# First FFN groups of both layers: un-normalized input, block products instead of direct ones

## The chip, the cores and the metric

The kernel runs on one core of a Trainium2 chip. The metric is the device time of one launch in microseconds (us); the time of a kernel is the median of its runs.

## The reference

One sequence of 512 tokens with 1024 channels passes two layers, all in float32. A layer is a mixer and a gated ConvFFN, each behind an RMS norm and each added to the residual `h`. The change touches the FFN and the way into it:

```python
def rms_norm(x, g):
    y = x * rsqrt(mean(x * x, axis=-1) + EPS)
    return y * g

def gated_conv_ffn(x, w_gate, w_up, conv_w, conv_b, w_down):   # D_FF = 2816
    g = einsum('bsd,df->bsf', x, w_gate)
    g = causal_dwconv3(g, conv_w) + conv_b        # 3 taps along the tokens, per channel
    up = einsum('bsd,df->bsf', x, w_up)
    return einsum('bsf,fd->bsd', silu(g) * up, w_down)

for layer in range(2):
    h = h + mixer(rms_norm(h, norm_mix[layer]))
    hn = rms_norm(h, norm_ffn[layer])
    h = h + gated_conv_ffn(hn, ...)
```

The factor of the norm is one number per token (`rstd`) and one per channel (`norm_ffn`). It commutes with a product over the channels as far as the token's number goes, so it can be applied to the outputs of `w_gate` and `w_up` instead of to their input.

## The kernel before

**Layout.** Channels lie on the 128 partitions and tokens along the free axis: `h[k]`, k = 0..7, is 128 channels by 512 tokens. For a float32-like result every operand is split into a high and a low half of type fp32r, and each product is three matmuls, high by high, high by low, low by high (`mm3`). The halves of the FFN's input are `hg[k]`, those of weights come from the pools `whi` and `wlo` (6 slots each) and are made from `raw` tiles (4 slots) that the SP queue fetches, 512 KB each. A high half is a rounding copy on ACT. A low half is a subtraction on DVE (`parts`, `halves`), or a negated copy on ACT and an accumulating DMA that POOL issues (`summed`, and kp = 2, 3 in `normalize`).

**Order of work.** The program is written in a tile framework: a planner with its own costs takes each engine's instructions in order of priority (the order of the program text) as their operands and slots become free, and writes one fixed order per engine. `behind` and `inorder` pin some of it. So PE's order also is not that of the text: of two groups of matmuls, the one that the planner sees ready goes first.

**Stages.** mixer 0, its output projection `oe` (two column groups `gi` of 96 matmuls), FFN 0, mixer 1, its output projection `oo`, FFN 1, final norm. `project` takes its residual output block by block: `done` adds a block to `h[k]`, and `Norm.add` makes `hg[k]` as the halves of `h[k]` times the norm weight, and adds the squares up on POOL (`ssq`). The FFN has 22 blocks of 128 hidden channels, taken in groups `f` of two blocks (gate and up, two blocks each). Groups run in parts, and after each part comes the down projection `d` (layer 1: `dn`) over its blocks:

```python
PARTS = (((0, 2), 0, 2), ((4,), 2, 6), ((6, 8), 6, 10), ((10, 12), 10, 14), ...)
```

**A direct group** (`direct`, f = 0 and 2): 4 outputs by 8 k by 3 = 96 matmuls of 512 columns. Group 0 works on `hg` not yet normalized: in its middle `rstd_cols` and `rstd_spread` make `r`, the tokens' `rstd` on all partitions, and its outputs are multiplied by `r` in `evacuate`. While it runs, `normalize(kp)` for the four pairs kp makes the normalized `hg` anew and, from it, the sums and differences of its four blocks (two channel halves by two token halves of 256), with their halves `t23` and `t41`.

**A group in block products** (`both`, all other f): gate and up, each as 7 products of 4 kp by 3 = 12 matmuls of 256 columns (a Strassen form; a plain product in blocks would take 8). Each of the 14 products needs its own stationary halves: `a11`, `s12`, `s34` and the two plain blocks through `summed`, seven slots a group. Results are put together out of PSUM banks a, e, b by copies on ACT and additions on DVE. Then come the convolution (one ACT and two DVE instructions a block), SiLU (ACT), the product with up (DVE) and the halves of the result, `a_hi` (ACT) and `a_lo` (DVE), which are the operands of `d`.

In layer 1 the residual is turned by PE at the start of the FFN (`turn_residual`, tiles `hT`, copied by ACT into `y`), and `t23` lies in the memory of `h`.

## Time and profile before

| what | value |
|---|---|
| median of 3 runs | 994.64 us (994.16 to 994.67) |
| the profiled execution's own time | 994.15 us |
| its span in the profile | 992.4 us |
| PE busy | 982.9 us (99%), 5905 matmuls |
| weight loads (PEld) busy | 875.6 us (88%) |
| DVE busy | 728.5 us (73%) |
| ACT busy | 536.3 us (54%) |
| POOL busy | 105.3 us (11%) |
| FFN 0 begins, first `gu` matmul | 146.13 us |
| FFN 1 begins, first `hT` transpose | 633.84 us |

A line of the profile's timeline has the start, the duration, the engine, the line of the code, the operation, the tiles out<-in, the shapes and a count. In square brackets is how long the engine was idle before, and what released it. A PE duration includes the pipeline, so the pace of matmuls is read from their starts.

### The profile page before, as it was taken

How to read it: one execution, taken by the hardware profiler on the slowest of the kernel's cores; microseconds unless marked ns; L12 is line 12 of the kernel's file. 1: busy time of each engine (PE TensorE's matmuls, PEld its weight loads, DVE VectorE, ACT ScalarE, POOL GpSimd, SP SyncE). 2: the span in 40 equal slices, each digit the busy share in tenths (PEclk: the TensorE clock that was granted, in tenths of full speed). 3: DMA queues.
4: the chain of work that ended last, by engine and by line, in shares of the span. 5: the costliest groups of instructions: out<-in, count | busy, mean ns of one | idle time of the engine just before them, and what ended most of it. 6: DMA issues, size and time to landing. Idle time of an engine off the chain costs nothing.

```text
span 992.4 us, 14934 instructions
## 1 busy us (share of the span) xinstructions
PE 982.9 (99%) x5905; PEld 875.6 (88%) x5905; DVE 728.5 (73%) x1104; ACT 536.3 (54%) x806; POOL 105.3 (11%) x121
## 2 busy tenths in 40 slices
PE   9999999999999999999999999999999999999997
PEld 6788888898999989999888988888989899898996
DVE  6897458967785877858988665399668768687676
ACT  5623346744653746537668634675546366363664
POOL 2141031200000000000300001211000010000100
PEclk9999999999999999999999999999999999999999
DMA  7442225544553645536423513435546456464542
GB/s 246 133 146 85 86 88 131 121 148 118 133 147 97 181 121 132 148 98 180 136 87 93 182 54 97 105 91 130 143 101 159 124 125 173 94 163 126 123 112 85
DMA packets 83073, 125.07 MB, mean 126 GB/s; under 512 B 4308, under 2 KB 56252, under 8 KB 83004
## 3 DMA queue, kind: packets, MB, share of 16 engines
q1 hardware_dynamic: 74028, 98.24, 31.4%
q0 software_dynamic: 7056, 23.60, 13.3%
q10 hardware_dynamic: 1920, 2.30, 0.7%
q8 instruction: 46, 0.75, 0.3%
q14 instruction: 23, 0.19, 0.1%
HBM read 98.42 MB, written 2.10 MB: 101 GB/s over the span
## 4 chain that ended last, share of the span: by engine, by line
PE 94%; issue 1%; DVE 1%; DMA 1%; ACT 0%; DVEq 0%; POOLq 0%; ACTq 0%
PE d L154 4%; PE d L153 4%; PE d L155 4%; PE dn L153 4%; PE dn L154 4%; PE dn L155 4%; PE gu L153 3%; PE gu L154 3%; PE gu L155 3%; PE v L153 1%; PE oo L155 1%; PE oo L153 1%; PE v L155 1%; PE oe L155 1%; PE oe L154 1%; PE v L154 1%
## 5 line engine op out<-in xcount | busy, mean ns | idle before, releaser
L153 PE MATMUL dn<-whi_dn,a_hi 128*128 128x512 f32 (+1 forms) x180 | 69.4, 386 | 0.0
L154 PE MATMUL dn<-wlo_dn,a_hi 128*128 128x512 f32 (+1 forms) x180 | 69.3, 385 | 0.0
L154 PE MATMUL d<-a_lo,whi_d 128*128 128x512 f32 x176 | 68.7, 390 | 0.0
L155 PE MATMUL d<-a_hi,wlo_d 128*128 128x512 f32 x176 | 68.5, 389 | 0.0
L155 PE MATMUL dn<-whi_dn,a_lo 128*128 128x512 f32 (+1 forms) x180 | 67.9, 385 | 0.0
L153 PE MATMUL d<-a_hi,whi_d 128*128 128x512 f32 x176 | 66.9, 390 | 0.0
L566 DVE SCALAR_TENSOR_TENSOR c<-rows,prm,c 128x512 f32<-128x512 f32 x88 | 66.4, 766 | 0.0
L141 POOL DMA_DIRECT2D wlo_g<-raw_g x22 | 19.1, 867 | 373.9 <-ACT wlo_g L140 257.9
L1109 DVE TENSOR_TENSOR y<-dn,y 128x512 f32<-128x512 f32 (+1 forms) x49 | 32.5, 674 | 23.3 <-PE dn L155 23.0
L140 ACT ACTIVATE wlo_g<-raw_g 128x1024 fp32r<-128x1024 f32 x22 | 23.2, 1056 | 42.4 <-PE dn L154 42.4
L572 ACT ACTIVATE s<-c,prm 128x512 f32<-128x512 f32 x44 | 31.7, 720 | 20.5 <-DVE c L566 20.4
L679 DVE TENSOR_TENSOR wlo_s34u<-s34u,whi_s34u 128x1024 fp32r<-128x1024 f32 x18 | 22.0, 1225 | 27.9 <-ACT whi_s34u L678 27.9
L155 PEld LDWEIGHTS dn<-whi_dn,a_lo 128*128 128x128 f32 x180 | 33.8, 188 | 7.3 <-DVE a_lo L262 0.2
L678 ACT ACTIVATE whi_s12u<-s12u 128x1024 fp32r<-128x1024 f32 x18 | 18.9, 1051 | 39.3 <-PE d L154 33.7
L153 PEld LDWEIGHTS dn<-whi_dn,a_hi 128*128 128x128 f32 x180 | 33.8, 188 | 7.0 <-ACT a_hi L260 0.2
L154 PEld LDWEIGHTS dn<-wlo_dn,a_hi 128*128 128x128 f32 x180 | 33.8, 188 | 6.4
L154 PEld LDWEIGHTS d<-a_lo,whi_d 128*128 128x128 f32 x176 | 33.1, 188 | 7.3 <-DVE a_lo L262 0.2
L305 DVE TENSOR_TENSOR h<-d,h 128x512 f32<-128x512 f32 x48 | 32.5, 683 | 9.2 <-PE d L155 9.2
L153 PEld LDWEIGHTS d<-a_hi,whi_d 128*128 128x128 f32 x176 | 32.8, 188 | 7.0
L155 PEld LDWEIGHTS d<-a_hi,wlo_d 128*128 128x128 f32 x176 | 33.0, 188 | 6.7
L260 ACT ACTIVATE a_hi<-s 128x512 fp32r<-128x512 f32 x44 | 27.6, 628 | 16.1 <-DVE s L751 7.4
L149 DVE TENSOR_TENSOR wlo_dn<-raw_dn,whi_dn 128x1024 fp32r<-128x1024 f32 x22 | 26.8, 1220 | 11.6 <-ACT whi_dn L148 11.6
(1274 smaller groups left out, 3469.1 us busy)
## 6 DMA issues: line engine op xcount, KB each, us to landing
raw_g<-in_w_ffn_gate_dram SPq DMA_DIRECT2D x36, 512.0 KB, 4.6
raw_u<-in_w_ffn_up_dram SPq DMA_DIRECT2D x36, 512.0 KB, 4.7
wlo_g<-raw_g POOLq DMA_DIRECT2D x22, 512.0 KB, 4.7
raw_d<-in_w_ffn_down_dram SPq DMA_DIRECT2D x22, 512.0 KB, 4.0
raw_dn<-in_w_ffn_down_dram SPq DMA_DIRECT2D x22, 512.0 KB, 4.0
wlo_u<-raw_u POOLq DMA_DIRECT2D x19, 512.0 KB, 4.6
raw_oe<-in_w_out_even_dram SPq DMA_DIRECT2D x8, 512.0 KB, 3.6
raw_g<-in_w_ffn_gate_dram SPq DMA_DIRECT2D x16, 256.0 KB, 2.9
```

The costliest lines, as they stand in the source:

```text
L140: first = nc.scalar.activation(lo, raw, AF.Copy, scale=-1.0)
L141: nc.gpsimd.dma_start(lo, raw, accum_op=ALU.add)
L149: behind(nc.vector.tensor_tensor(lo, raw, hi.bitcast(F32), ALU.subtract), after[0])
L153: nc.tensor.matmul(ps, lhs[0], rhs[0], start=start, stop=False)
L154: nc.tensor.matmul(ps, lhs[0], rhs[1], start=False, stop=False)
L155: nc.tensor.matmul(ps, lhs[1], rhs[0], start=False, stop=stop)
L260: nc.scalar.activation(hi, src, AF.Copy, scale=scale)
L305: nc.vector.tensor_tensor(h[k], ps, h[k], ALU.add)
L566: nc.vector.scalar_tensor_tensor(c, t[:, i : S + i], prm("cf", i * NF + ft), c, op0=ALU.mult, op1=ALU.add)
L572: nc.scalar.activation(s, c, AF.Silu, bias=self.prm("bf", ft))
L679: nc.vector.tensor_tensor(lo, src, hi.bitcast(F32), ALU.subtract)
L1109: nc.vector.tensor_tensor(dst, ps, dst, ALU.add)
```

## The change

`normalize` goes. In both layers the FFN's products take `hg`, residual times norm weight, to the end, and `r` is applied to outputs in every group. Group 0 keeps its gate direct (48 matmuls of 512) and takes up in 7 block products (84 of 256). Group 2 becomes a group in block products. The weights of group 0 are fetched and prepared from within `project`, ahead of the matmuls of its second column group. In the block sums kp = 0 and 3 go by DVE and kp = 1 and 2 by the accumulating DMA.

```diff
-    def project(name, w, acts, ks, norm, before=None):
+    def project(name, w, acts, ks, norm, before=None, between=None):
...
+            if gi == 1 and between is not None:
+                between()
...
+    def first_weights(layer, into):
+        w = w_ffn_gate[layer][:, : 2 * P].rearrange("(h k p) c -> p h k c", h=2, p=P)
...
+        into["g", 0] = parts(*gate[0])
...
+        halves(w[0][:, 0], w[1][:, 0], r0[:, :, :P])
+        put((2, 4), *parts(*raws["u", 1]))
+        nc.vector.tensor_tensor(a22, a21, a22, ALU.add)
+        nc.vector.tensor_tensor(a21, a11, a21, ALU.subtract)
+        nc.vector.tensor_tensor(a11, a22, a11, ALU.subtract)
+        nc.vector.tensor_tensor(a12, a12, a11, ALU.subtract)
+        put((3, 5), *parts(r1, 4, 2 * P, f"u{layer}_0_s41"))
+        into["g", 1] = parts(*gate[1])
+        put((6, 7), *summed(r0, 4, 2 * P, f"u{layer}_0_s23"))
...
-        def normalize(self, kp):
-            for i, k in enumerate((kp, kp + NP)):
-                nc.vector.scalar_tensor_tensor(x[:, i, :], h[k], self.prm("ffn", k), r, ...)
-            halves(hg[kp], x[:, 0, :])
-            halves(hg[kp + NP], x[:, 1, :])
+        def block_sums(self, kp):
+            nc.scalar.activation(t[:, 2:, :], h[kp]..., AF.Copy, scale=self.prm("ffn", kp))
...
+            for (hi, lo), src in ((self.t41[kp], t[:, 2:, :]), (self.t23[kp], t[:, :2, :])):
+                if kp in (0, 3):
+                    self.summed = halves(hi, lo, src)
                     continue
...
+        def first_up(self, s):
+            for product in (1, 2, 3, 5, 6, 7, 4):
+                ps = self.multiply(banks, f"u{n}", product, self.weights["u", product],
+                                   "c" if product == 3 else None)
...
-        def both(self, f):
+        def products(self, f):
...
-                if (key, product) == ("g", 4):
-                    s[1] = self.silu(self.conv(pads[1], f + 1), f + 1)
-                elif (key, product) == ("g", 3):
-                    s[0] = self.silu(self.conv(pads[0], f), f)
+                if (key, product) in (("g", 4), ("g", 3)):
+                    j = product == 4
+                    row = pads[j][:, 2:]
+                    nc.vector.tensor_tensor(row, row, self.r, ALU.mult)
+                    s[j] = self.silu(self.conv(pads[j], f + j), f + j)
+                    if j:
+                        nc.vector.tensor_tensor(s[1], s[1], self.r, ALU.mult)
...
+            nc.vector.tensor_tensor(kept[:, :2, :], kept[:, :2, :], self.r..., ALU.mult)
             nc.vector.tensor_tensor(s0, kept[:, :2, :], s0, ALU.mult)
...
         def hidden(self, f, before=lambda i, j: None):
+            if f > 0:
+                self.products(f)
+                return
...
+            evacuate = self.first_gate(first)
+            for kp in range(NP):
+                self.block_sums(kp)
+            self.first_up(evacuate())
```

`between` is `first_weights`; its up products stand in the order 1 (`a11`), 2 and 4, 3 and 5, 6 and 7, and only the last pair goes through the accumulating DMA. `block_sums` takes one scaled copy on ACT and four DVE instructions of 256 columns a pair kp, two of which multiply `h[kp + NP]` by its norm weight in passing. In `first_up` products 1, 3 and 7 are copied by ACT and 2, 5, 6 and 7 bring an addition on DVE. `rstd_cols` now stands at step (3, 0) of the gate's matmuls and `rstd_spread` at (4, 1).

`first_gate` is `direct` for the two gate outputs alone; its `evacuate` multiplies by `r` on DVE before the convolution and on POOL after the SiLU, as before. In layer 1 the eight turns of the residual, formerly ahead of the first eight of 32 steps, come ahead of the first eight of 16.

## The prediction

> **What bounds the kernel now.** I read the page first, for the engines' shares and the chain.

> ```profile
> span 992.4 us, 14934 instructions
> ...
> PE 982.9 (99%) x5905; PEld 875.6 (88%) x5905; DVE 728.5 (73%) x1104; ACT 536.3 (54%) x806; POOL 105.3 (11%) x121
> ...
> PE 94%; issue 1%; DVE 1%; DMA 1%; ACT 0%; DVEq 0%; POOLq 0%; ACTq 0%
> ```

> PE carries the chain. A busy PE need not be at its pace, so the waits of PE come next:

> ```profile
> PE clock L62 <- DVE idle L57: 1.3, 1, 1.3
> PE u_20b L535 <- DMA wlo_u<-raw_u: 0.8, 1, 0.8
> PE z L415 <- ACT hgh L392: 0.4, 1, 0.4
> ```

> 2.5 us in all. So there are two ways to change the time: fewer or shorter matmuls, or new waits of PE. The pace is in the timeline of PE (a 512-column run) and in the chain (products of 12):

> ```profile
> 157.08 0.39 PE L153 MATMUL gu<-hgh,whi_u 128*128 128x512 f32 x1
> ...
> 170.23 0.39 PE L154 MATMUL gu<-hgl,whi_g 128*128 128x512 f32 x1
> ```

> ```profile
> 264.25 1.44 PE g_8a L535 x12
> 265.69 1.44 PE u_8a L535 x12
> ...
> 270.01 1.44 PE u_8e L535 x12
> ```

> 58 steps from 157.08 to 170.23 are 0.2267 us for a matmul of 512; 1.44 / 12 is 0.1200 us for one of 256, more than half of the other. That eats much of what seven products instead of eight save. Last, the engines that feed PE, by stretches (down projection 222 to 244, group 6, group 8; then all of the two direct groups):

> ```profile
> 222.11:243.90 21.79, 21.79 (x98) 17.92 (x97) 18.01 (x29) 8.01 (x10) 0.86 (x1) 1.00 0.52 141
> 243.95:264.08 20.13, 20.13 (x169) 20.13 (x168) 12.54 (x20) 11.20 (x18) 1.70 (x2) 1.00 0.37 91
> 264.08:284.31 20.23, 20.23 (x170) 20.20 (x169) 15.49 (x24) 14.43 (x24) 0.85 (x1) 1.00 0.64 176
> ```

> ```profile
> 146.00:191.00 45.00, 45.00 (x206) 37.30 (x205) 37.60 (x66) 30.69 (x47) 10.54 (x10) 1.00 0.51 117
> ```

> After length and PE come PEld, DVE, ACT, POOL. DVE has 46.0 of 62.2 us in a whole part and 37.6 of 45 in the direct groups: room, but at single joints little of it. Two joints in DVE's timeline:

> ```profile
> 268.33 1.22 DVE L679 TENSOR_TENSOR wlo_s12u<-s12u,whi_s12u 128x1024 fp32r<-128x1024 f32 x1
> ...
> 289.83 0.68 DVE L262 TENSOR_TENSOR a_lo<-s,a_hi 128x512 fp32r<-128x512 f32 x1
> ```

> The first ends at 269.55; the product that needs it (u_8e) starts at 270.0. The second ends at 290.5, while `d` runs from 284.3: 24 matmuls over blocks 6 and 7 and three over 9 (27 x 0.2267 = 6.1) cover it to 290.4. And where such a joint is missed now, in the last group of layer 1 (chain):

> ```profile
> 942.24 6.62 issue
> ...
> 948.88 5.94 DMA wlo_u<-raw_u
> ...
> 954.86 1.46 PE u_20b L535 x10
> ```

> The accumulating DMA went out 6.85 us after its group began (942.03); in group 8, which has no wait, it is 5.7 us (269.78 after 264.08).

> **PE's work.** Group 2: 96 x 0.2267 = 21.76 becomes 168 x 0.1200 = 20.16, 1.60 less. Up of group 0: 48 x 0.2267 = 10.88 becomes 84 x 0.1200 = 10.08, 0.80 less. 2.40 a layer, 4.80 in all, and 2 x (36 + 72) = 216 matmuls more. The transposes and the small products for `rstd` stay. I take no error on the paces, since thousands of matmuls keep them. [...]

> **The start of the FFN** (layer 0, from T = 146.13). Gate takes 48 x 0.2267 + 1.17 (`ssc` 0.81, `ssr` 0.36) = 12.05; products 1, 2, 3 need only `hg`. So the sums `t41` are due at T + 16.4 (product 5), `t23` at T + 17.8 (6), group 2 starts at T + 22.1. Ready: the last `hgl` ends at T + 2.7 (148.12 + 0.75). The sums no longer wait for `rstd`, for which DVE idled 2.05 us at 154.4. By the distances of starts (256 columns 0.34, 512 0.60, 1024 1.13) DVE needs 16 x 0.34 + 4 x 0.60 + 1.13 for the gate's second low half + about 1 for `rstd` = 10.0, so it ends at T + 12.7. The pairs by DMA: kp 2 summed at about T + 9, copy 0.6, issue 0.9, landing 4.2 (median on the page), T + 14.7, due with its half of product 5 at T + 17.1: 2.4 us of slack. Of the weights, two slots of six are free when `oe`'s second group starts, and one comes free at 129.8, 135.2, 145.4 and 146.1 as before; the gate's second half gets the fifth, ready near T + 3, due at T + 6.3. The moved DMAs keep their place behind `oe`'s on SP. On POOL the accumulate for products 6 and 7 (0.86) stands near the last `ssq` addition (148.77 to 150.06), for which PE's `ssc` waits at 150.21; two such issues stand around it now (146.96, 150.01), so I charge nothing; in the worst order it is 0.9.

> Then DVE has, up to product u5 of group 2 (T + 27.9): gate outputs 2 x (0.60 + 2 x 0.66), additions 4 x 0.34, the end of up 2 x 0.34 + 3 x 0.60, `a11` 1.2, `s12` of both 2 x 2.33: 13.5 us in 15.2. ACT has about 26 us by T + 35. In layer 1 eight copies of `hT` (0.52 each, 4.2) come on top, while PE's turns put the due times off by 3.5. DVE worked as tightly from 181 to 205 us before, and PE waited nowhere. So 0 to 1.9 us a layer: the upper end uses up the slack by the 2.8 us that ACT waited for DVE's sum at 165.45 and a landing of 5.94 instead of 4.2. I take 0.3, 0.6 in all. A gain beyond PE's has no room: PE does not wait here now.

> **The multiplications by rstd.** Four DVE instructions of 512 columns, 2.4 us, in each of ten groups a layer. DVE's total: +54 busy (80 x 0.68), -23 (normalizing, 16 of each kind at 0.74 and 0.68), about +34 for the new sums and halves: near 793. In a part it is 46.0 + 4.8 of 62: not the bound. First groups of a part prepare during `d`, where DVE idles. Second groups (eight) prepare behind the first group's end, with 0.4 us of slack at u5: 2.4 us late, unless g2 and g7, whose weights are ready (DMA issued 261.6; low half done 267.1), go ahead of it; they give 2.88. Bounds 0 and 1.07 (the pause at u_20b, 0.97 + 0.10, where the joint slipped by 1.15): I take 0.15, as seven of eight joints show under 0.1: 1.2 in all.

> The ten joints from products to `d`: the last `a_lo` comes 1.2 to 2.4 us later. Ready besides: block 9 for three more outputs (9 x 0.2267 = 2.0), and three of the seven banks for the next column group (18 x 0.2267 = 4.1). Bounds 0 and 2.3 each; I take 0.

> **Sum.** -4.8 + 0.6 + 1.2 = -3.0. Against the profiled execution's 994.15 (span 992.4, 1.75 around it) that is 991.15; the median of the runs lies 0.49 above it, so 991.6.

> **Rivals.** (a) *The chain to `d` grows and PE's order doesn't make room.* Place: all ten joints. Two of the four multiplications lie in the last block's own chain, 1.2 us; past a slack of about 0.2 that is 1.0 each: -4.8 + 1.8 + 10 = +7.0, 1001.6. It decides from 0.3 us a joint. For it: the slack is nil as ordered. Against: PE already fills 6 us there, with work to spare. 0.18. (b) *Second groups slip as u_20b did*, all eight by 1.07 (one is there already): -4.8 + 0.6 + 7.5 = +3.3, 997.9. For it: that joint, slipped by half of the 2.4. Against: g2 and g7. 0.10. (c) *The start is late* by 1.9 in both layers: -4.8 + 3.8 + 1.2, 994.8. 0.14. (d) *The pace follows the columns*, 113.3 ns: 19.04 a group, 8.2 saved, 988.2 with the same charges. The rows do not bear it out: 0.02. [...]

> **How the numbers follow.** The forecast has 0.56; its own range is 989.8 (no charge) to 992.6. A measurement can tell about 0.2%, 2.0 us: faster is below 992.65, slower above 996.6. Faster: forecast and (d), 0.58. Same: (c), 0.14. Slower: (a) and (b), 0.28. The range runs from 989.3 (no charge, and half of the 1.07 at u_20b gone) to 1000.0, which takes in (c) and (b) and a joint of 0.8 us in (a), and leaves out the rest of (a) and (d), not quite 0.2.

> **What would show it.** 6121 matmuls, PE busy near 979, DVE near 793. Group 2 begins 22 us after FFN 0's first gate matmul and `d` over blocks 0 and 1 is reached 42.3 after it (44.95 before). PE's waits should name at most `t` or `t23` in the start, `wlo_s12u` or `wlo_u` in second groups, `a_lo` at `d`. Waits of 0.3 us and more at each `d` would prove (a); a start of 46 us would prove (c) and worse.

## The result, and the profile after

The changed kernel takes 1021.75 us (median of 6 runs, 1018.81 to 1024.28), the kernel before 994.65 beside it: a ratio of 1.0274 (95% interval 1.0256 to 1.0292). The profiled execution took 1021.34, 27.19 more than that of before (994.15).

The page after, its head and the chain:

```profile
span 1019.6 us, 15474 instructions
...
PE 990.4 (97%) x6121; PEld 886.2 (87%) x6121; DVE 786.2 (77%) x1210; ACT 548.6 (54%) x828; POOL 109.3 (11%) x123
...
PE 21%; issue 5%; DMA 4%; DVE 2%; ACT 1%; POOLq 0%; DVEq 0%; ACTq 0%; SPq 0%
```

The matmuls are the 6121 that were counted, and DVE is 7 us under what was forecast; PE is busy 11 us more than the 979 that were forecast. And the chain, 94% PE before, now breaks up among other engines. PE's waits say where (engine, what waited, for what: us in all, times, longest):

```profile
PE g_4b L539 <- DMA wlo_g<-raw_g: 3.3, 2, 1.9
PE u_2b L539 <- DMA wlo_u<-raw_u: 2.6, 2, 1.6
PE v L153 <- ACT v L987: 2.2, 1, 2.2
PE u_2a L539 <- DVE wlo_a L556: 1.5, 1, 1.5
...
PE g_4e L539 <- DVE wlo_s12g L556: 1.2, 2, 0.7
PE u_2e L539 <- ACT whi_s12u L555: 1.0, 2, 0.8
PE u_20b L539 <- DMA wlo_u<-raw_u: 1.0, 2, 0.6
PE u_16b L539 <- DMA wlo_u<-raw_u: 0.9, 2, 0.4
```

Group 2 and group 4 wait for their weights' halves, every second group for `wlo_u`, and `v` in mixer 1, whose code is the same, for ACT. No wait at `d` or `dn` is longer than 0.51.

One more thing is new. The view by windows gives the granted clock behind the columns of the engines. In the changed kernel it is 0.50 in two stretches of 3.41 us; before it is 1.00 from 5.2 to 985.4, as long as matmuls run:

```profile
216.90:220.30 3.40, 3.40 (x18) 3.40 (x18) 1.23 (x1) 1.42 (x2) 0.00 (x0) 0.50 1.11 205
534.35:537.75 3.40, 3.40 (x10) 2.62 (x9) 3.40 (x6) 3.40 (x8) 0.00 (x0) 0.50 0.00 0
```

In them matmuls of 256 columns start 0.213 us apart instead of 0.120, those of 512 0.427 instead of 0.227, so 1.5 to 1.6 us of each are lost. They begin right behind waits of PE: 0.42 at `u_4e` and 1.32 at `g_4b` in the 3.4 us ahead of the first, 2.21 at `v` ahead of the second.

Where the 27.2 us lie is read from PE's timeline, stage by stage. "Start" runs from group 0's first gate matmul to `d` over blocks 0 and 1, "4" from there to `d` over blocks 2 to 5 (so it holds 10.9 us of `d`, and group 4), "parts" from there to `v` or to the end of the last matmul. All are us of the profiled execution.

| kernel | start 0 | 4 | parts | mixer 1 | start 1 | 4 | parts, end | median of runs |
|---|---|---|---|---|---|---|---|---|
| before | 44.95 | 31.03 | 270.81 | 141.27 | 48.13 | 31.03 | 272.21 | 994.65 |
| after | 49.89 | 35.77 | 274.26 | 145.33 | 51.16 | 34.89 | 275.43 | 1021.75 |
| e1 no multiplications | 50.41 | 31.67 | 270.75 | 142.00 | 51.01 | 31.96 | 271.06 | 1003.99 |
| e2 group 2 direct | 52.65 | 31.03 | 274.96 | 142.76 | 53.09 | 31.03 | 274.44 | 1013.72 |
| e3 up direct | 45.45 | 31.06 | 274.85 | 142.69 | 48.52 | 31.06 | 275.63 | 1004.69 |
| e4 both direct | 44.91 | 31.03 | 275.09 | 142.53 | 48.13 | 31.03 | 275.87 | 1003.34 |
| e5 order in mixer 1 | 50.59 | 34.53 | 273.97 | 141.17 | 50.98 | 34.98 | 275.15 | 1016.70 |
| e11 both forms, all orders | 50.45 | 37.29 | 271.82 | 141.24 | 53.11 | 36.43 | 273.86 | 1018.13 |
| e12 up direct, all orders | 43.84 | 31.60 | 272.08 | 141.20 | 48.26 | 31.55 | 272.96 | 994.90 |
| e13 e11, gate's tail late | 43.47 | 34.43 | 271.85 | 141.19 | 46.10 | 35.51 | 274.03 | 1001.69 |
| e14 e12, SiLU behind | 43.82 | 31.60 | 271.76 | 141.23 | 46.76 | 31.55 | 273.06 | 995.22 |

After less before: 4.94 + 4.74 + 3.45 + 4.06 + 3.03 + 3.86 + 3.22 = 27.30, and 0.09 ahead of the first start. (The profiled execution of e12, 996.65, is the slowest of its ten, so its row adds up to more than its median.)

Half clock lies in other rows too, and makes them up to 1.6 us longer for each such stretch: the mean clock was 0.97 in start 0 of e1 and of e2 (1.00 before and after), and over the executions of e2, e5 and e11 0.995, 0.996 and 0.994 (before 0.998, after 0.995).

### The profile page after: what moved, and what is told of

The parts are those of the page before. It is cut to its first block, busy times and chain, and to the rows that moved or that the text cites. A ratio compares the mean times of both kernels' runs of the same rounds, so it can differ in the third digit from the quotient of the medians.

```text
span 1019.6 us, 15474 instructions
## 1 busy us (share of the span) xinstructions
PE 990.4 (97%) x6121; PEld 886.2 (87%) x6121; DVE 786.2 (77%) x1210; ACT 548.6 (54%) x828; POOL 109.3 (11%) x123
## 5 line engine op out<-in xcount | busy, mean ns | idle before, releaser
L153 PE MATMUL dn<-whi_dn,a_hi 128*128 128x512 f32 (+1 forms) x180 | 69.9, 388 | 0.6 <-ACT a_hi L260 0.5
L154 PE MATMUL dn<-wlo_dn,a_hi 128*128 128x512 f32 (+1 forms) x180 | 69.3, 385 | 0.0
L154 PE MATMUL d<-a_lo,whi_d 128*128 128x512 f32 x176 | 68.6, 390 | 0.0
L153 PE MATMUL d<-a_hi,whi_d 128*128 128x512 f32 x176 | 65.5, 392 | 0.1
L1156 DVE TENSOR_TENSOR y<-dn,y 128x512 f32<-128x512 f32 (+1 forms) x49 | 32.6, 678 | 14.2 <-PE dn L155 13.6
L556 DVE TENSOR_TENSOR wlo_s34u<-s34u,whi_s34u 128x1024 fp32r<-128x1024 f32 x20 | 24.5, 1226 | 24.3 <-ACT whi_s34u L555 24.3
L153 PEld LDWEIGHTS dn<-whi_dn,a_hi 128*128 128x128 f32 x180 | 33.8, 188 | 8.6 <-ACT a_hi L260 2.2
L140 ACT ACTIVATE wlo_g<-raw_g 128x1024 fp32r<-128x1024 f32 x20 | 21.1, 1057 | 35.8 <-PE dn L154 35.8
L612 ACT ACTIVATE c<-rows,prm 128x512 f32<-128x512 f32 x44 | 31.3, 715 | 16.9 <-DVE rows L791 16.1
L153 PEld LDWEIGHTS d<-a_hi,whi_d 128*128 128x128 f32 x176 | 32.7, 188 | 7.8 <-ACT a_hi L260 1.3
L154 PEld LDWEIGHTS dn<-wlo_dn,a_hi 128*128 128x128 f32 x180 | 33.9, 188 | 6.4
L260 ACT ACTIVATE a_hi<-s 128x512 fp32r<-128x512 f32 x44 | 27.4, 628 | 22.0 <-DVE s L801 19.6
L154 PEld LDWEIGHTS d<-a_lo,whi_d 128*128 128x128 f32 x176 | 33.0, 188 | 7.0 <-DVE a_lo L262 0.2
L141 POOL DMA_DIRECT2D wlo_u<-raw_u x21 | 18.1, 860 | 174.0 <-ACT wlo_u L140 142.8
L209 POOL TENSOR_TENSOR ssq_f<-ssq_f,sq_f 128x512 f32<-128x512 f32 x14 | 19.4, 1388 | 141.7 <-ACT sq_f L208 106.8
```

Source lines behind the costliest of these rows:

```text
L140: first = nc.scalar.activation(lo, raw, AF.Copy, scale=-1.0)
L141: nc.gpsimd.dma_start(lo, raw, accum_op=ALU.add)
L153: nc.tensor.matmul(ps, lhs[0], rhs[0], start=start, stop=False)
L154: nc.tensor.matmul(ps, lhs[0], rhs[1], start=False, stop=False)
L260: nc.scalar.activation(hi, src, AF.Copy, scale=scale)
L556: nc.vector.tensor_tensor(lo, src, hi.bitcast(F32), ALU.subtract))
```

## Experiments

The theories at the outset: A, the start has too little cover for the preparation of groups 2 and 4; B, the multiplications by `rstd` cost; C, mixer 1 and the clock are on their own.

**Which part of the change costs (e1 to e4).** e1 leaves out the three multiplications in `products` (the first runs for both blocks, so these are four instructions a group):

```diff
-                    nc.vector.tensor_tensor(row, row, self.r, ALU.mult)
...
-                        nc.vector.tensor_tensor(s[1], s[1], self.r, ALU.mult)
...
-            nc.vector.tensor_tensor(kept[:, :2, :], kept[:, :2, :],
-                                    self.r.rearrange("p (a b) -> p a b", a=2), ALU.mult)
```

> The changed kernel without the three DVE instructions per products group that apply rstd (row of gate j=0 and j=1, s[1], kept): those 512-column multiplications, about 0.6 us each, 96 us of DVE in nothing but 10 groups a layer x 2.4 us = 48 us, are left out, so the outputs of groups 2 to 20 lack rstd. Changed kernel: 1021.75 us. Theory A (the start of the FFN and group 4 have too little cover for their preparation): the two starts stay at 49 to 51.5 us and group 4 loses at most the 2.4 us of group 2's own multiplications, parts come back from 63.0 to about 62.3: 1010 to 1016. Theory B (the multiplications delay DVE everywhere, and the late DMAs, group 4 and mixer 1 follow from that): parts 62.2, group 4 20.2, mixer 1 141, starts 47: about 1000. Theory C (clock and mixer 1 are on their own): mixer 1 stays near 145.

1003.99. The parts are back (270.75 and 271.06), group 4 nearly; the starts are not. So the multiplications are the whole of the parts' 6.7 us, and group 4 and mixer 1 are worse with them. The starts are as theory A had them, the time is nearer to B's.

e2 puts group 2 back to direct matmuls, e3 group 0's up, e4 both; all stay un-normalized:

```diff
-            if f > 0:
+            if f == 2:
+                self.direct(2, ((0, 1), (2, 3)), self.ch)()    # e2, e4
+            elif f > 0:
                 self.products(f)
...
-            evacuate = self.first_gate(first)
+            rest = self.direct(0, (range(4),), self.weights, first)    # e3, e4
```

> The changed kernel with group 2 as 96 direct matmuls of 512 columns on the input not normalized, its outputs multiplied by rstd; group 0's up stays in products. PE work 3.2 us more than in the changed kernel. Theory A (group 2 in products is what lacks cover): starts 44.2 to 45, group 4 20.2 to 21, parts 63.0 as in the change: 1000 to 1005. Theory B (multiplications): group 4 and parts as in the change, only part of the start back: 1012 to 1018. Theory A' (up of group 0 in products is what lacks cover): starts stay at 49 or more: above 1015.

> The changed kernel with group 0's up as direct matmuls (48 of 512 columns, all four outputs of group 0 in one sweep as before), group 2 in products. PE work 1.6 us more than in the changed kernel. Theory A (group 2 in products): as late as the change, 1018 to 1024. Theory A' (up in products): about 1005 to 1010. Theory B: as the change less the work of up's own additions, 1018 to 1022.

> Never normalized alone: groups 0 and 2 both direct on the input not normalized, rstd on the outputs of all groups, the first weights fetched from inside the output projection as in the change. PE work as before, 4.8 us more than in the changed kernel. Theory A: starts 44.7, group 4 20.2, parts 62.3 to 63.0: 996 to 1003. Theory B (multiplications): 1008 to 1015, as group 4, parts and mixer 1 stay late. Theory C (mixer 1 lost its 4 us to something that neither product form touches): mixer 1 stays at 145 here too.

1013.72, 1004.69 and 1003.34. Never normalizing alone costs 1003.34 - 994.35 (before, in the same runs) = 9.0 us. To that, group 2's products add 1.35, up's add 10.4, and both together 18.4, each net of the work that PE saves by them. Theory A was right about the place and wrong about the part: with up of group 0 direct, group 2's products cost next to nothing. The times of the theories were not hit closely: e2 lies above A's range, e3 and e4 0.3 off the ends of A' and A. In e3 and e4 the mean clock of layer 0's group 4 is back at 1.00, from 0.95 in the change, and over the executions at 0.998 and 0.997, from 0.995. One caution: in e2 the start is longer than in the change, and PE waits there for the accumulating DMAs of the block sums (3.6 us for `t23l` alone), as ACT copies group 2's direct weights ahead of them; the mean clock of start 0 is 0.97 there. So the 10.4 have a cause of their own, and e2 does not show why up's products cost in the change.

**Mixer 1 (e5).** In the changed kernel DVE stands at the first subtraction on `raw_u` until its fetch has landed, with the normalization behind it (DVE's timeline, the bracket is idle time and its end's cause); PE then waits:

```profile
518.34 0.16 DVE L250 SCALAR_TENSOR_TENSOR rc_m1c<-ms_m1c,rc_m1c 128x4 f32<-128x4 f32 x1
522.79 1.23 DVE L945 TENSOR_TENSOR raw_u<-raw_u,raw_u 128x1024 f32<-128x1024 f32 x1 [4.29 <-DMA raw_u<-in_w_in_odd_dram]
```

```profile
533.68 0.50 PE L153 MATMUL v<-whi_v,hgh 128*128 128x512 f32 x1 [2.21 <-ACT v L987]
```

SP issued that fetch 9.0 us after `v` began (515.15 and 506.14), before 4.1 (497.03 and 492.92).

```diff
-                    nc.vector.tensor_tensor(b12, b12, b11, ALU.subtract)
+                    behind(nc.vector.tensor_tensor(b12, b12, b11, ALU.subtract), normed[2])
```

> The changed kernel, with one order pinned in mixer 1: DVE's first subtraction on raw_u stands behind the low half of the first pair's sums in normalize, no longer ahead of the whole normalization. Nothing is left out. In the changed kernel DVE stands 4.29 us at that subtraction until raw_u has landed, PE then waits 2.2 us in v, and a stretch of 3.41 us at half clock follows. Theory C (mixer 1's 4.06 us are a DVE queue blocked at its head by a late fetch, and the dip follows from PE's wait): mixer 1 back to 141 to 142, one dip instead of two, 1017.5 to 1018.5. Rival (v's input is late for another reason, ACT or the clock by itself): mixer 1 at 144 to 145, the second dip stays, 1021.

1016.70. Mixer 1 is 141.17, the wait at `v` and the half clock behind it are gone:

```profile
534.00:540.00 6.00, 6.00 (x28) 4.98 (x27) 6.00 (x9) 5.52 (x9) 0.87 (x1) 1.00 0.47 90
```

The queue is the cause, as theory C had it, and the clock follows the wait. But mixer 1 is not on its own: in e1 to e4, which do not touch it, it is 142.0 to 142.8 and not near 145. Why the late work at the end of FFN 0 puts off the fetch was not tried by itself.

**The start: three single causes, and all orders at once (e6, e9, e10, e11).** e6 makes all sums' halves on ACT and DVE; e9 moves the gate's two multiplications from POOL to DVE; e10 prepares up's weights for products 6 and 7 after the first block sums; e11 has e9, e10, e5 and the order of e7 below at once.

```diff
-                if kp in (0, 3):
+                if True:                                            # e6
...
-                    nc.gpsimd.tensor_tensor(s, s, self.r, ALU.mult)
+                    nc.vector.tensor_tensor(s, s, self.r, ALU.mult)  # e9
...
                 self.block_sums(kp)
+                if kp == 0:
+                    self.weights["later"]()    # e10: put((6, 7), *summed(...))
```

> The changed kernel with the sums of all four pairs kp halved by ACT and DVE; the four accumulating DMAs a layer for kp 1 and 2 are gone, DVE gets 4 x 0.60 us more in each start, ACT 4 x 0.52 less. Nothing is left out. Theory S (up's products in group 0 wait for the accumulating DMAs, and DVE for the slots that these hold: 3.41 us idle): starts from 49.9 and 51.2 to 46 to 47, group 4 with d from 35.8 and 34.9 to 33 or less: 1010 to 1014. Rival D (it is DVE's and ACT's amount of work in the start, not the DMAs): the start stays at 49 to 51 or grows by up to 2.4: 1020 to 1026.

> The changed kernel with the two multiplications of group 0's gate by rstd on DVE (2 x 0.60 us) instead of POOL (1.9 to 2.1 us each, during which two DVE instructions of 0.68 us took 1.99 and 1.78, and behind which the DMA for group 2's wlo_g waited on POOL's queue). Nothing is left out. Theory P (this POOL stretch holds up group 2's wlo_a and wlo_g, and group 4's preparation behind them): both starts 1.5 to 2.5 shorter, group 4 with d 1 to 2 shorter: 1014 to 1018. Rival D (DVE's queue is full in the start, and 1.2 us more on it is as bad): 1020 to 1023.

> The changed kernel with up's last weights of group 0 (products 6 and 7: two ACT copies of 0.95 us and the accumulating DMA) prepared after the first pair's block sums, no longer ahead of them from inside the output projection. Nothing is left out. In the changed kernel ACT makes three weight copies between the last two blocks of hgh, and the block sums begin at 150.3 instead of 146.9 (e3), with up's products waiting at their end. Theory Q (the moved weights push the sums back, 3 us at each start): starts 47 to 48, 1013 to 1017. Rival D (DVE's amount of work up to group 2 sets the end, whenever the sums begin): less than 1 us a start, 1019 to 1023; worse if products 6 and 7 now wait for the DMA.

> The changed kernel with everything found so far: e5's order in mixer 1, e7's order of the second groups (not in layer 1's last part), e9's and e10's edits. Both product forms are in. Nothing is left out. If the orders are all: e8's 999.55, less 2.4 for the last part, less 1.6 for up's products, 995 to 997. If up in products costs the start whatever the order: starts stay at 46 to 50 and group 4 at 33 or more: 1001 to 1008.

1020.92, 1023.27, 1024.50 and 1018.13: none mends the start. Each time the rival came nearer; e9, e10 and e11 even lie above its numbers. In e10 the sums do begin earlier (147.93 instead of 150.29), and the start is as long, 50.03. A caution here too: start 0 ran at a mean clock of 0.97 in e6 (1.00 in the change), and e10's execution at 0.990 (0.995), so the length of a start alone could hide a gain of up to 1.6 us. DVE's timeline is less open to this. It gives the end of the block sums' last low half on DVE and the begin of `wlo_s12g`, the low half of group 2's first sum of weights (us from group 0's first gate matmul; layer 0, layer 1):

| kernel | block sums end | `wlo_s12g` begins | start |
|---|---|---|---|
| after | 19.36, 19.72 | 25.32, 28.98 | 49.89, 51.16 |
| e6 | 18.61, 19.33 | 26.03, 27.38 | 50.13, 51.47 |
| e10 | 16.92, 18.80 | 26.49, 31.17 | 50.03, 53.04 |
| e11 | 16.88, 18.81 | 27.25, 31.27 | 50.45, 53.11 |
| e12 | 14.74, 20.10 | 15.86, 21.81 | 43.84, 48.26 |
| e13 | 15.05, 18.81 | 21.44, 25.12 | 43.47, 46.10 |

In e6, e10 and e11 the block sums end earlier and `wlo_s12g` mostly comes later still: what stands between the two decides. That left DVE's queue as a whole. Its timeline in the changed kernel, from the idle time on:

```profile
162.95 0.69 DVE L709 TENSOR_TENSOR s12g<-raw_g,raw_g 128x512 f32<-128x512 f32 x1 [3.41 <-DMA t<-t]
...
165.49 1.28 DVE L642 TENSOR_TENSOR rows<-gu,rstd_f 128x512 f32<-128x512 f32 x2
...
167.02 0.68 DVE L556 TENSOR_TENSOR wlo_a<-raw_g,whi_a 128x512 fp32r<-128x512 f32 x1
167.62 2.73 DVE L614 SCALAR_TENSOR_TENSOR c<-rows,prm,c 128x512 f32<-128x512 f32 x4
...
170.60 0.68 DVE L556 TENSOR_TENSOR wlo_a<-raw_u,whi_a 128x512 fp32r<-128x512 f32 x1
...
171.53 1.99 DVE L556 TENSOR_TENSOR wlo_s12g<-s12g,whi_s12g 128x1024 fp32r<-128x1024 f32 x1
```

and in e12, with up direct (the same lines have other numbers there):

```profile
161.18 0.69 DVE L556 TENSOR_TENSOR wlo_a<-raw_g,whi_a 128x512 fp32r<-128x512 f32 x1
161.78 0.68 DVE L556 TENSOR_TENSOR wlo_a<-raw_u,whi_a 128x512 fp32r<-128x512 f32 x1
162.38 1.22 DVE L556 TENSOR_TENSOR wlo_s12g<-s12g,whi_s12g 128x1024 fp32r<-128x1024 f32 x1
...
168.47 1.28 DVE L627 TENSOR_TENSOR rows<-gu,rstd_f 128x512 f32<-128x512 f32 x2
...
171.06 2.73 DVE L598 SCALAR_TENSOR_TENSOR c<-rows,prm,c 128x512 f32<-128x512 f32 x4
```

With up direct, gate and up end together at 170.2, so gate's evacuation and convolution come behind group 2's preparation. With up in products gate ends at 159.4, and the same instructions go ahead of it: `wlo_s12g` is made 9.15 us later. Of these, 4.31 are the later end of the block sums, 3.85 gate's evacuation and convolution, and 0.99 three additions of up's products.

**Gate's tail behind (e13).** On e11: group 2's preparation is written before gate's convolution, its first sum pinned behind the block sums, and up's `kept` gets its own memory.

```diff
-                    s = self.silu(self.conv(t, j), j)        # in evacuate
...
+            self.ready[2] = self.prepare(2)                  # in first_up, after the products
+            for j in range(2):
+                s[j] = self.silu(self.conv(s[j], j), j)
```

> The kernel of e11 (both product forms, orders mended, 1018.1), with group 0's gate convolution, SiLU and multiplication by rstd written after group 2's preparation (and after up's products), group 2's first sum s12g pinned behind the block sums' last low half, and a memory of its own for up's kept. Nothing is left out. In e11 DVE stood 2.98 us at s12g for a slot, then did 6 us of gate's evacuation ahead of group 2's wlo_a and s12g. Theory O (in products, up lets gate end 10 us earlier, and gate's tail goes ahead of group 2's preparation in DVE's queue; with up direct both end together and the tail comes behind it): starts 44 to 46 instead of 50.5 and 53.1, group 4 nearer 33: 1000 to 1008. Rival W (DVE's amount of work up to group 4 is what is too much, in any order): what the start gains comes back at d or in group 4: 1014 to 1020.

1001.69, 16.4 less than e11. The convolution now stands behind `wlo_s12g`, as in e12:

```profile
168.18 1.22 DVE L556 TENSOR_TENSOR wlo_s12g<-s12g,whi_s12g 128x1024 fp32r<-128x1024 f32 x1
...
173.72 2.73 DVE L615 SCALAR_TENSOR_TENSOR c<-rows,prm,c 128x512 f32<-128x512 f32 x4
```

The starts are 43.47 and 46.10, 1.5 and 2.0 under before, and the mean clock of the execution is 0.999, in e11 0.994. Theory O holds. The three parts of the edit were not run one by one, but layer 1 tells two of them apart: there the block sums end at 18.81 in e11 and in e13, and in e11 `s12g` stood behind them without a pin, yet `wlo_s12g` comes 6.15 us earlier and the start is 7.0 shorter. So there it is not the pin; what the memory for `kept` adds is not shown. What is left lies in group 4, 3.4 and 4.5 us: its first sum and the second stand 14.2 us apart in DVE's queue, with group 2's tail, its multiplications and seven additions of `d` to `h` between them, where `d` covers 10.9 us:

```profile
186.81 0.69 DVE L708 TENSOR_TENSOR s12g<-raw_g,raw_g 128x512 f32<-128x512 f32 x1 [1.04 <-DMA raw_g<-in_w_ffn_gate_dram]
...
201.01 0.68 DVE L710 TENSOR_TENSOR s12g<-s12g,raw_g 128x512 f32<-128x512 f32 x1
```

ACT waits for that sum, with the negated copy for `wlo_g` queued behind, whose DMA PE then waits for at `g_4b` (0.79 in layer 0, 1.95 in layer 1; in the changed kernel ACT waits 5.36 there in layer 0, and PE 1.32 and 1.93):

```profile
201.79 1.06 ACT L555 ACTIVATE whi_s12g<-s12g 128x1024 fp32r<-128x1024 f32 x1 [4.16 <-DVE s12g L710]
...
203.01 1.06 ACT L140 ACTIVATE wlo_g<-raw_g 128x1024 fp32r<-128x1024 f32 x1
```

**The parts (e7, e8, e12, e14).** Why 2.4 us on DVE cost 0.83 of PE is seen on ACT. Before (group 8 begins at 264.08):

```profile
266.13 0.73 ACT L572 ACTIVATE s<-c,prm 128x512 f32<-128x512 f32 x1
...
268.45 1.04 ACT L140 ACTIVATE wlo_u<-raw_u 128x1024 fp32r<-128x1024 f32 x1
```

and in e4 (begins at 264.51):

```profile
269.10 0.72 ACT L603 ACTIVATE s<-c,prm 128x512 f32<-128x512 f32 x1 [2.44 <-DVE c L597]
...
270.25 1.04 ACT L140 ACTIVATE wlo_u<-raw_u 128x1024 fp32r<-128x1024 f32 x1
```

ACT waits for the convolution, which the multiplications put off, and the negated copy for `wlo_u` waits behind that SiLU: 5.74 us into the group instead of 4.37. The DMA and `u_8b` follow. e7, on e3, writes the second group's preparation ahead of the first group's SiLU:

```diff
+            if f in (6, 10, 14, 18):
+                self.ready[f + 2] = self.prepare(f + 2)
+            s[1] = self.silu(s[1], f + 1)
```

> The kernel of e3 (up of group 0 direct, 1004.7), with the preparation of each part's second group written ahead of the first group's SiLU and multiplications by rstd in the program: ACT's negated copy for the second group's wlo_u now stands ahead of the second SiLU, and DVE's s34u and wlo_s12u ahead of the multiplications. Nothing is left out. Theory H (the multiplications cost 0.83 us a part because ACT waits for DVE's convolution with wlo_u's copy queued behind): the eight parts go from 63.0 to 62.2 to 62.4: 998 to 999. Rival (DVE's amount of work, wherever it stands: then d waits for a_lo instead): parts stay at 63 or more, 1003 to 1010.

e8 adds e5's order and e9's edit; e12 leaves e7's order out of layer 1's last part; e14 pins both SiLU behind the negated copy.

> The kernel of e7 with e5's order in mixer 1, and the two multiplications of group 0's gate by rstd on DVE instead of POOL (2 x 0.6 us instead of 2 x 2 us; DVE stood 2.9 us for them, and u_2a's bank with it). Nothing is left out. PE's work is 3.2 us under that of the kernel before. If H, C and this wait are what is left: 994.65 - 3.2 + 0 to 2 = 991.5 to 993.5, faster than before. If the multiplications are a matter of DVE's amount of work: 1000 or more.

> The kernel of e8 (up of group 0 direct, group 2 in products, orders mended) without e7's order in layer 1's last part, where u_20b waited 3.0 us for its DMA, landing after 8.7 us beside the fetches of final_norm and of dn. Nothing is left out. Theory: that part back from 66.0 to about 64: 997 to 998. Rival: the wait comes from the multiplications there too and stays: 999 to 1000.

> The kernel of e12 (up of group 0 direct, group 2 in products, 994.9), with ACT's two SiLU of a first group pinned behind the negated copy for the second group's wlo_u. Nothing is left out. In e8 and e12 PE leaves each u_8b (u_12b, ...) after 5 of 12 matmuls for another product and comes back, 0.28 us a part. Theory: with the copy ahead of both SiLU seven parts come back to 62.2: 993 to 993.5. Rival (PE's order is the planner's, which still takes the DMA for late, or d now waits for a_lo): 994.5 to 996.

e7 1004.22, where H had 998 to 999: the parts fall from 63.0 to 62.48, nearly as H said, but in the last part `u_20b` waits 2.8 us, and the mean clock falls to 0.995, from 0.998 in e3. e8 999.55, where 991.5 to 993.5 was hoped for: there that DMA took 8.7 us to land, with the fetches of `fin` and `dn` beside it. e12 994.90, ratio to before 1.0011 (1.0001 to 1.0020): H holds for the parts, mostly 62.48 again, and past the program's start no wait of PE in it is over 0.72. e14 995.22, 1.0014 (1.0004 to 1.0023), no gain that can be told.

**What was tried on top (e15 to e18).** e15 pins s12g in e14 behind the sums, as in e13; e16 pins PE's product 7 of up behind 2, e17 all products in the text's order, e18 product 2 of up behind 6.

```diff
+                if (key, product) == ("u", 2) and f in (8, 12, 16, 20):
+                    behind(mms[at], self.last6)              # e18
```

> The kernel of e14 with group 2's first sum s12g pinned behind the block sums' last low half as well (in e3 DVE stood 1.71 us there for a slot held until an accumulating DMA landed). Nothing is left out. Theory S for the start with up direct: layer 1's start from 48.3 to 47, layer 0's stays at 43.8: 1 to 1.5 under e14. Rival: the same as e14 within 0.5, as the start has slack there.

> The kernel of e14 (up of group 0 direct, group 2 in products, orders mended, 995.2) with PE's product 7 of up pinned behind its product 2 in the groups from 4 on, so that PE no longer leaves u_8b (u_12b, ...) after 5 of 12 matmuls. Nothing is left out. Theory (PE's leaving and coming back is all that the 0.27 us a part are, the DMA is in time): eight parts from 62.48 to 62.2: 992.5 to 993.5, level with or just faster than before. Rival (the DMA for wlo_u is really late by that much): the same 0.27 or more as a wait at u_8b: 995 to 996.5.

> The kernel of e14 with all 14 products of each group pinned in the order of the text on PE. Nothing is left out. Theory: as e16, and group 4 with d from 31.6 to 31.1 in both layers: 991.5 to 992.5. Rival (a product that comes late now holds the others up): waits of 0.5 us and more at group 2 and 4, 995 to 1000.

> The kernel of e14 with PE's product 2 of up pinned behind its product 6 in the second groups 8, 12, 16 and 20 (in e14 and e16 product 6 stood inside product 2, and product 7 inside gate's product 4; e16 had pinned the wrong pair). PE's order in these groups is now product by product. Nothing is left out. Theory (0.24 us a part are lost where PE leaves a product and comes back): eight parts from 62.48 to 62.25, 993.3 to 993.7, 0.1% under e14, level with before. Rival (product 6 or 2 then waits for its weights by as much): 995 to 996.5 as e14.

998.31, 995.49, 1033.74 and 997.56. The theory missed in all four. e15 moves the loss to group 4 of layer 1 (34.70). e16 pinned a pair that stood so already. In e17 PE waits 3.2 us for ACT's `kept` at each of `u_8a`, `u_12a`, `u_16a` and `u_20a` of layer 0, in e18 0.4: products taken in order meet data that really is late, so the 0.27 us a part are not PE's order alone. No form of the change was below the kernel before.

## Why the prediction was wrong

**PE's work, -4.8: right as far as it shows.** Where little else is late, most of it is seen: e13's starts are 1.5 and 2.0 under before, for 2.4 each counted, and e14's, with group 2 alone in products, 1.1 and 1.4 for 1.6.

**The start, +0.6: the step that failed.** It is 4.94 + 2.4 = 7.3 in layer 0 and 3.03 + 2.4 = 5.4 in layer 1, 12.8 in all, where the bound was 1.9 a layer. The sums were to end at T + 12.7; the last low half ended at 165.57, T + 19.35: begun at T + 4.1 instead of 2.7, as ACT made three weight copies ahead of the last `hgh`, 0.86 of idle at `rstd`, and 3.41 at `s12g`, whose slot was held until an accumulating DMA of the block sums had landed. The forecast had counted slack for products 5 and 6 and none for slots. But this lateness is not what decides: in e10 the sums end 2.4 us earlier for nothing, and in e13 they end at T + 15.05 and 18.81, also later than forecast, with starts below those of before. What failed is the count "13.5 us in 15.2": there is room for the work, as e13 shows, and it was taken for granted that DVE does it in the order in which it falls due. The written order put gate's tail first, 3.85 us of evacuation and convolution and then its other work, and e13, which puts it behind, gains the starts back (with the reserve on `kept` made there).

**Group 4, not in the sum: 8.6.** The prediction named `d` over blocks 0 and 1 only as a due time, and not as group 4's cover. DVE comes to it late from the start, and has 10.9 us of `d` for group 2's tail and group 4's preparation together. e2, e3 and e4 all have 31.0 to 31.1 here, so it takes both forms; and it takes the multiplications, as e1, with both forms and without these, loses only 1.6 of the 8.6. A stretch at half clock, about 1.5, is in it. e13, with the starts mended, still loses 7.9. Whether another order would mend this too was not tried.

**The second groups, +1.2: the mechanism was near, the size was off.** The parts cost 6.7, about 0.83 at each joint: rival (b), given 0.10. The check that failed was of the wrong instruction: it followed DVE to `wlo_s12u`, and the wait runs from DVE's convolution to ACT's SiLU to the copy behind it. That g2 and g7 go ahead does not help a product, u2, whose own weights are late.

**The ten joints to `d`, 0: right.** Rival (a) had no place: the list of waits has one for `a_hi`, of 0.51.

**Mixer 1, not in the sum: 4.1.** It was held untouched. The order that the planner had fixed there held for the old time of arrival of the fetch (4.1 us into `v`) and not for the new one (9.0), and about 1.6 of the 4.1 are the clock.

**The sum** with what was measured, PE's -4.8 as counted: -4.8 + 12.8 + 8.6 + 6.7 + 4.1 = +27.4.

## What to carry to other kernels

Where an edit makes one group of results ready earlier, ask what its follow-up work now stands in front of: here DVE and ACT served their queues in the written order, and a step that was not yet needed blocked one that was (e13: 16.4 us). When instructions are added to one engine, follow the engine that waits for it, and what is queued there behind the waiting instruction, to the DMA at the end. Undo each part by itself and both: the costs do not add (1.35, 10.4, together 18.4), and the part that was watched least was the dear one. And read each such run's trace, since leaving a part out can bring a wait of its own, as in e2.

## What the runs showed of the hardware

An accumulating DMA of 512 KB took 5.3 us to land in the median for `wlo_u` (4.6 before), and 8.7 in e8 beside transfers on two other queues. And while POOL multiplied (170.53 to 174.67), two DVE instructions beside it took 1.99 and 1.78 us instead of 1.22 and 0.68; e9, without these POOL multiplications, was not faster (1023.27).
